# Weights split ahead in an encoder layer: stores and loads on another engine's queue

## The chip, the cores and the metric

One core of a Trainium2 chip. The metric is the device time of one run in microseconds (us). The engines are TensorE (PE in the profile, with PEld for its weight loads), VectorE (DVE), ScalarE (ACT), GpSimd (POOL) and SyncE (SP). SyncE here does nothing but issue transfers; each engine works through its own instructions in order and waits on semaphores for the others.

## What is computed

One layer of an encoder in float32, from the reference:

```python
u      = x @ W_in                        # rq, rk, rv, rg (4 x 512), aq (512), ak, av (2 x 128)
# group R: two-directional retention, 8 heads of 64, chunks of 64 here: scores * decay^|i-j|,
#          chunk states carried forward and backward, group norm per head, swish gate
# group A: windowed attention, 8 query heads on 2 key heads, +-128 tokens, sink logit, ALiBi
mix    = concat(R, A) @ W_out
h      = LN1(alpha * x + mix)
f      = SwiGLU(h) + sigmoid(h @ W_pg) * (p @ W_pe)     # FFN width 2816, p is 256 wide
out    = LN2(alpha * h + f)                             # x: (1, 1024, 1024) float32
```

## The kernel before

All large products run on TensorE as three products of operands that were split in two: `hi` is the value rounded to TensorE's reduced float32 format, `lo` is the rest, and the sum is hi·hi + hi·lo + lo·hi (`mm3`, lines L82, L83, L84). So each weight must be split before it is used: ScalarE copies `hi`, VectorE subtracts to get `lo`. For the projection weights this happens just before use (L76 and L77, with a raw tile of which there are two in flight, loaded by SyncE on L116). `w_out`, `w_pg`, `w_pe` and `p` are needed later in the kernel. They are loaded, combined, split and written back to DRAM in the shadow of the mixers: that is `presplit_out`, `presplit_gate` and `presplit_small`. Each of their steps is a `put`: ScalarE copies (L653), VectorE subtracts (L654), and a transfer of 512 KB stores both parts (L655). There are 28 puts for `w_out` (to `wod`), 28 for `w_pg` (to `pgd`), 4 for `p` (`ptd`) and 4 for `w_pe` (`ped`). A put writes into one of two operand tiles (`pro`, or `aq` and `y` tiles that are free at the time), which must be stored before a later put may reuse it.

The mixers take four head pairs in turn. First the attention of pair 0, then the retention of pair 0, then for pairs 1, 2 and 3 retention and attention together. The order of TensorE's instructions is written out by hand: `run` walks a list of steps, and each `F` in it takes its share of a queue of projection steps (one step, or tick, is three matmuls of 512 columns) that belong to the next pair. The order on ScalarE, VectorE, GpSimd and SyncE comes from a scheduler that places instructions by its own estimate; `behind` ties an instruction behind the latest projection step. Work with a due time stands in the lists `later` and `side` and is issued when the count of ticks reaches it. For pair 1 to 3 a phase has 48 ticks.

The steps that the prediction speaks of:

- `keys` (K(0), K(1)): TensorE transposes, then four ScalarE copies scaled by the decay per half (L424), into the tiles `qq` and `pt`.
- `kv` (C(0), C(1)): TensorE forms 64x64 products of decayed keys and values (L439); ScalarE (L448) and VectorE (L446) copy them out of PSUM.
- `decay_k`: for one head ScalarE makes two exponentials in a tile `sq` (L388), of which there is one; GpSimd multiplies by masks (L390) and adds (L391) into `dt`.
- `norm` (M(0), M(1)): TensorE sums squares (L528), VectorE scales the row (L530), and then, 3, 6, 9, 12 and 15 ticks later, the chain: SyncE spreads the row over partitions (L535), GpSimd raises to the power -1/2 (L538), SyncE stores to DRAM (L541), SyncE fetches it back spread (L545), VectorE scales the output with it (L549). The small tile `sn` exists once, so the second half waits for the first.
- attention: scores (L577, L578 on TensorE, L579 on VectorE, L582 on ScalarE), transposes (L617) and their copies (L622), a small copy of the denominators (L599).

In a phase every load and every store goes through SyncE's one queue, those of the norm chain and those of the puts alike; GpSimd has the masks and the powers.

Of the kernel before, what the change touches and what calls it, by code (L numbers as in the profile page):

```python
# [47 lines left out]
def layer(tc, xT, xn, w_first, w_mt, w_rv, w_out, w_pg, w_pe, pT, w_gu, w_dn,  # L48
# [89 lines left out]
    def bt(shape, tag, bufs=None, dt=F32):  # L138
        return bpool.tile(list(shape), dt, tag=tag, bufs=bufs, name=nm(tag))
# [243 lines left out]
            behind(act.activation(qd[:, h, :], cst[:, C_QD:C_QD + CH], AF.Exp, scale=lq[:, 2 * i + h:2 * i + h + 1]))  # L383

    def decay_k(i, h):
        e = bt([P, 2, CH], "sq", 1)
        for d in range(2):
            behind(act.activation(e[:, d, :], cst[:, C_B64:C_B64 + CH], AF.Exp,  # L388
                                  scale=lg[:, 8 * d + 2 * i + h:8 * d + 2 * i + h + 1]))
        pool.tensor_tensor(e, e, masks, ALU.mult)  # L390
        pool.tensor_tensor(decays[i][1][:, h, :], e[:, 0, :], e[:, 1, :], ALU.add)  # L391
# [260 lines left out]
    def put(x, o, dst):  # L652
        behind(act.activation(o[:, 0, :], x, AF.Copy))  # L653
        behind(dve.tensor_tensor(o[:, 1, :], x, o[:, 0, :].bitcast(F32), ALU.subtract))  # L654
        sp.dma_start(dst, o.bitcast(F32))  # L655

    def presplit_small(n, ops, start, at0, at1, raw=None):

        hold = []

        def load():
            r = rawt(2 * HF) if raw is None else raw
            hold.append(r)
            if n < 2:
                for j in range(4):
                    sp.dma_start(r[:, j * 2 * P:(j + 1) * 2 * P], pT[4 * n + j])
            else:
                sp.dma_start(r, w_pe[n - 2])

        def step(j):  # L670
            o = ops[j]() if callable(ops[j]) else ops[j]
            put(hold[0][:, j * HF:(j + 1) * HF], o, ptd[2 * n + j] if n < 2 else ped[n - 2, j])

        return [(ticks[0] + at, f) for at, f in ((start, load), (at0, lambda: step(0)), (at1, lambda: step(1)))]

    def presplit_out(kt, ops, start, gap, raws=()):


        hold = []

        def load():
            for j in range(2):
                r = raws[j] if j < len(raws) else rawt(2 * HF)
                sp.dma_start(r, w_out[kt + 4 * j])
                hold.extend([r[:, :HF], r[:, HF:]])

        def step(p, k, k2, i):
            x, o = hold[k], ops[i % len(ops)]
            if k2 is not None:
                behind(dve.tensor_tensor(x, x, hold[k2], ALU.add))  # L690
            put(x, o() if callable(o) else o, wod[p - 1, kt])

        todo = ((1, 0, None), (2, 2, None), (3, 3, None), (5, 0, 1), (7, 1, 3), (6, 0, 3), (4, 0, 2))
        at = gap if isinstance(gap, tuple) else [start + 5 + gap * i for i in range(7)]
        return [(ticks[0] + start, load)] + [(ticks[0] + at[i], lambda i=i, a=a: step(*a, i)) for i, a in enumerate(todo)]

    def presplit_gate():

        first, other = ([a_tile([P, 2, HF], "pre", t) for _ in range(2)] for t in ("A1", "A0"))
        ops = [a_tile([P, 2, HF], "pro", "A1", F32R) for _ in range(2)]  # L700
        n = [0]

        def load(k):
            for j in range(2):
                sp.dma_start((other if k == 1 else first)[j], w_pg[j, k])

        def steps(k):
            raw = other if k == 1 else first

            (a11, a21), (a12, a22) = ([raw[j][:, i, :] for i in range(2)] for j in range(2))  # L710

            def s(p, x, *sums):
                def f():
                    for a in sums:
                        behind(dve.tensor_tensor(*a))
                    put(x, ops[n[0] % 2], pgd[p - 1, k])
                    n[0] += 1
                return f

            return [s(1, a11), s(4, a22), s(2, a12), s(5, a22, (a22, a21, a22, ALU.add)),  # L720
                    s(7, a21, (a21, a11, a21, ALU.subtract)), s(6, a11, (a11, a22, a11, ALU.subtract)),
                    s(3, a12, (a12, a12, a11, ALU.subtract))]

        load(0)
        load(1)
        k0, k1, k2, k3 = map(steps, range(4))
        k1[0] = pair_of(k1[0], lambda: load(2))
        k3[0:0] = [lambda: load(3), lambda: None]
        at = [2 + 2.8 * k for k in range(14)] + [60 + 1.9 * k for k in range(7)] + [73 + 1.9 * k for k in range(9)]
        return [(ticks[0] + t, f) for t, f in zip(at, k0 + k1 + k2 + k3, strict=True)]  # L730
# [60 lines left out]
    with tc.manual_schedule(engines={mybir.EngineType.PE}):  # L791
# [25 lines left out]
        for i in range(1, NPAIR):  # L817
            assert i == 1 or not side, len(side)
            r = Retention(i, ytile(2 * i), states)
            a = Attention(i, ytile(2 * i + 1))  # L820
            if i == 2:
                late = [ytile(6), ytile(7)]
                ops = [twin(late[1].bitcast(F32R)), twin(bt([P, S], "aq", 3, F32R))]
                side.extend(presplit_out(2, ops, 2, 3.4, late[:1]))
                side.extend(presplit_small(0, ops[::-1], 24, 31, 34.4) + presplit_small(1, ops[::-1], 31, 37.8, 41.2))
            elif i == 3:
                op = twin(bt([P, S], "aq", 3, F32R))
                rkx = bt([P, S], "rk", 2)
                more = []

                def spare_op(k):
                    if not more:
                        more.append(twin(bt([P, S], "rk", 2, F32R)))
                    return more[0] if k % 2 else op

                side.extend(presplit_out(3, [op, op, op, op, lambda: spare_op(1), op, lambda: spare_op(1)], 3,
                                         (8, 13.5, 19, 24.5, 30, 33.5, 37), [rkx]))
                side.extend(presplit_small(2, [op, lambda: spare_op(1)], 40, 43.5, 46.5, rkx))
                side.extend(presplit_small(3, [op, lambda: spare_op(1)], 46, 50, 53))
            G = [(f, i + 1, *x) for f, x in ((decay_q, ()), (decay_k, (0,)), (decay_k, (1,)))] if i + 1 < NPAIR else \  # L840
                [(lambda: None,)] * 3
            run([K(0), F, K(1), sco(0), F, *V, C(0), C(1), F, sco(1), S_(0, 0), F, trn(0), sco(2), S_(0, 1), F, trn(1),
                 sco(3), S_(1, 0), F, val(0), val(1), S_(1, 1), F, trn(2), sco(4), F, trn(3), sco(5), Q(0), F, val(2), val(3),
                 (r.scores,), F, trn(4), sco(6), Q(1), F, trn(5), sco(7), F, (r.out,), E(0), E(1), F, G[0], F, M(0), G[1], F,
                 val(4), val(5), G[2], F, trn(6), M(1), F, trn(7), F], 48)
            V = [val(6), val(7)]
# [1223 lines left out]
```

## Time and profile before

| | |
|---|---|
| time, median of 3 runs | 1168.02 us (1165.01 to 1168.27) |
| the profiled execution | 1168.96 us, span 1167.2 us |
| granted clock of TensorE | 0.998 |
| hardware queue (SyncE, ScalarE) | 200.11 MB, 49.6% of 16 engines |
| software queue (GpSimd) | 17.31 MB, 8.4% |

The span is the time from the first to the last instruction; 1.76 us lie around it. A row of a timeline gives start, duration, engine, line, operation, output and inputs by the program's names, a count, and in brackets the idle time of that engine before it with what released it. Names in the profile have no buffer numbers. SPq and POOLq are the two engines' issuing of transfers; "to landing" is the time from the issue to the arrival of the last byte.

The attention of pair 0 runs from about 33 to 118 us, the retention of pair 0 to about 160 us, pairs 1, 2 and 3 to about 345 us, and everything after the mixers from 360 us on.

### The profile page before, as it was taken

The page shows a single profiled execution, that of the slowest core. Times are in us where ns is not written, and L with a number is a line of the kernel's source. Part 1 is how long each engine was busy: PE and PEld are TensorE (multiplying, and loading weights), DVE is VectorE, ACT ScalarE, POOL GpSimd, SP SyncE. Part 2 cuts the span into 40 slices and gives each one's busy share as a digit, 9 for nine tenths or more (in the row PEclk, how much of TensorE's full clock was granted, in tenths as well). Part 3 has the DMA queues.
Part 4 walks back from the last instruction along what each step waited for, and adds up shares of the span by engine and source line. Part 5 has one row for each costly group of instructions (what it writes and reads, how often), then busy time and mean ns, then how long its engine had stood idle before and what let it go on. Part 6 is the DMA issues. An engine that isn't in the chain of part 4 may idle for free.

```text
span 1167.2 us, 19086 instructions
## 1 busy us (share of the span) xinstructions
PE 1151.9 (99%) x6978; PEld 965.8 (83%) x6978; DVE 895.7 (77%) x1687; ACT 564.4 (48%) x1162; POOL 105.1 (9%) x118
## 2 busy tenths in 40 slices
PE   9999999999999999999999999999999999999997
PEld 7888878777888888888888888888888888888886
DVE  5556678594858898948999988888888876774778
ACT  5645367666546366214444433443344445552462
POOL 2000010102010021000000000000000011124242
PEclk9999999999999999999999999999999999999999
DMA  6346777666567955756322332332223289999978
GB/s 251 103 159 214 258 241 232 211 210 194 154 216 241 365 178 185 269 193 210 112 96 98 115 107 98 103 134 101 100 73 136 83 249 344 348 236 217 256 172 233
DMA packets 88863, 218.64 MB, mean 187 GB/s; under 512 B 12544, under 2 KB 20928, under 8 KB 88768
## 3 DMA queue, kind: packets, MB, share of 16 engines
q1 hardware_dynamic: 79984, 200.11, 49.6%
q0 software_dynamic: 8784, 17.31, 8.4%
q8 instruction: 55, 0.90, 0.3%
q14 instruction: 40, 0.33, 0.1%
HBM read 143.35 MB, written 62.19 MB: 176 GB/s over the span
## 4 chain that ended last, share of the span: by engine, by line
PE 89%; issue 4%; DMA 3%; DVE 2%; ACT 1%; SPq 1%; POOL 0%; DVEq 0%; POOLq 0%; ACTq 0%
PE bmm L875 8%; PE bmm L874 8%; PE bmm L876 8%; PE bt L874 6%; PE bt L875 6%; PE bt L876 6%; PE bmm L82 4%; PE bmm L84 4%; PE bmm L83 4%; PE bs L876 4%; PE bs L875 4%; PE bs L874 4%; PE bo L876 4%; PE bo L875 4%; PE bo L874 4%
## 5 line engine op out<-in xcount | busy, mean ns | idle before, releaser
L82 PE MATMUL bmm<-H,w 128*128 128x512 f32 x240 | 97.2, 405 | 0.1
L84 PE MATMUL bmm<-H,w 128*128 128x512 f32 x240 | 94.0, 392 | 0.5 <-issue 0.5
L83 PE MATMUL bmm<-H,w 128*128 128x512 f32 x240 | 94.0, 392 | 0.0
L1474 ACT ACTIVATE ev<-ev 128x512 f32<-128x512 f32 x42 | 26.5, 630 | 105.0 <-DVE ev L1503 91.8
L1648 POOL DMA_DIRECT2D h0b<-in_w_dn x24 | 21.6, 900 | 537.7 <-DVE ev L1454 503.6
L82 PEld LDWEIGHTS bmm<-H,w 128*128 128x128 f32 x240 | 45.2, 188 | 12.2 <-issue 1.9
L84 PEld LDWEIGHTS bmm<-H,w 128*128 128x128 f32 x240 | 45.0, 188 | 10.2
L83 PEld LDWEIGHTS bmm<-H,w 128*128 128x128 f32 x240 | 45.1, 188 | 7.8
L582 ACT ACTIVATE sc<-sc,st 128x384 f32<-128x384 f32 (+1 forms) x64 | 37.3, 586 | 17.1 <-DVE st L579 17.0
L579 DVE CUSTOM_DVE_ANT_0 sc<-cst,bs,nskb 128x384 f32<-128x384 f32 (+1 forms) x64 | 35.2, 575 | 7.0 <-PE bs L578 6.9
L1503 DVE TENSOR_TENSOR ev<-ev,bt 128x512 f32<-128x512 f32 x44 | 30.0, 682 | 12.5 <-PE bt L876 12.5
L622 ACT ACTIVATE ptr<-bt 128x384 f32<-128x384 f32 (+1 forms) x64 | 26.5, 456 | 25.5 <-PE bt L617 25.4
L1454 DVE TENSOR_TENSOR ev<-ev,bs 128x256 f32<-128x256 f32 x63 | 25.5, 416 | 15.6 <-PE bs L876 14.7
L1476 DVE TENSOR_TENSOR ev<-ev 128x512 f32<-128x512 f32 x42 | 29.0, 691 | 10.5 <-ACT ev L1474 9.0
L77 DVE TENSOR_TENSOR w<-raw,w 128x512 fp32r<-128x512 f32 x34 | 23.0, 687 | 17.3 <-ACT w L76 16.7
L874 PE MATMUL bmm<-H,u 128*128 128x512 f32 x92 | 36.1, 392 | 0.0
L875 PE MATMUL bmm<-H,u 128*128 128x512 f32 x92 | 36.0, 392 | 0.0
L876 PE MATMUL bmm<-H,u 128*128 128x512 f32 x92 | 35.8, 389 | 0.0
L874 PE MATMUL bmm<-H,w 128*128 128x512 f32 x84 | 32.9, 392 | 0.0
L875 PE MATMUL bmm<-H,w 128*128 128x512 f32 x84 | 32.9, 392 | 0.0
L876 PE MATMUL bmm<-H,w 128*128 128x512 f32 x84 | 32.7, 389 | 0.0
L1454 DVE TENSOR_TENSOR ev<-ev,bo 128x256 f32<-128x256 f32 x70 | 28.3, 416 | 5.2 <-PE bo L876 4.5
(832 smaller groups left out, 3836.8 us busy)
## 6 DMA issues: line engine op xcount, KB each, us to landing
ad<-ev SPq DMA_DIRECT2D x33, 512.0 KB, 2.6
pgd<-pro SPq DMA_DIRECT2D x28, 512.0 KB, 3.3
raw<-in_w_gu SPq DMA_DIRECT2D x22, 512.0 KB, 4.0
ln<-in_w_gu SPq DMA_DIRECT2D x22, 512.0 KB, 4.6
raw<-ad SPq DMA_DIRECT2D x40, 256.0 KB, 6.2
ln<-ad SPq DMA_DIRECT2D x37, 256.0 KB, 6.3
H<-in_w_dn SPq DMA_DIRECT2D x33, 256.0 KB, 9.2
wod<-aq SPq DMA_DIRECT2D x16, 512.0 KB, 2.7
```

The costliest lines, as they stand in the source:

```text
L82: pe.matmul(o, lh, rh, start=start, stop=False)
L83: pe.matmul(o, lh, rl, start=False, stop=False)
L84: recent[0] = pe.matmul(o, ll, rh, start=False, stop=stop).ins.name
L579: dve.tensor_tensor_reduce(sc[g][:, :nk], cst[:, tc0:tc0 + nk], b[:, :nk], slope(i, g), nskb[:, 2 * i + g:2 * i + g + 1], ALU.add, ALU.min ...
L582: act.activation(sc[g][:, :nk], sc[g][:, :nk], AF.Exp, bias=st_[:, 0, j, g:g + 1], scale=-1.0, accum_out=st_[:, 2, j, g:g + 1])
L622: act.activation(p_[:, :hi - lo, :], tb[:, :hi - lo, :], AF.Copy)
L874: pe.matmul(o, lh, rh, start=start, stop=False, skip_group_check=True)
L875: pe.matmul(o, lh, rl, start=False, stop=False, skip_group_check=True)
L876: pe.matmul(o, ll, rh, start=False, stop=stop, skip_group_check=True)
L1454: dve.tensor_tensor(out_, x, b, ALU.add)
L1476: dve.tensor_tensor(c[:, 1, :], c[:, 0, :], c[:, 1, :], ALU.mult)
L1503: dve.tensor_tensor(get(name), ev[left][:, m, :], right, ALU.add)
```

## The change

The change has four parts. The stores of all puts and the loads of `w_out`, `w_pg`, `p` and `w_pe` are issued by GpSimd instead of SyncE. The two heads' exponentials of a pair go into halves of one `sq` tile. The loads of `p` and their puts come later in pair 2's phase. In pair 1's phase, where no steps of an earlier pair are left over (`V` is empty), one more `F` stands behind K(1), so the 48 ticks are shared by 21 of them instead of 20.

```diff
     def decay_k(i, h):
-        e = bt([P, 2, CH], "sq", 1)
+        if h == 0:
+            decays["e"] = bt([P, 2, 2, CH], "sq", 1)
+        e = decays["e"][:, h]
         for d in range(2):
             behind(act.activation(e[:, d, :], cst[:, C_B64:C_B64 + CH], AF.Exp, ...
...
     def put(x, o, dst):
         behind(act.activation(o[:, 0, :], x, AF.Copy))
         behind(dve.tensor_tensor(o[:, 1, :], x, o[:, 0, :].bitcast(F32), ALU.subtract))
-        sp.dma_start(dst, o.bitcast(F32))
+        pool.dma_start(dst, o.bitcast(F32))
...
             if n < 2:                                   # presplit_small: load
                 for j in range(4):
-                    sp.dma_start(r[:, j * 2 * P:(j + 1) * 2 * P], pT[4 * n + j])
+                    pool.dma_start(r[:, j * 2 * P:(j + 1) * 2 * P], pT[4 * n + j])
             else:
-                sp.dma_start(r, w_pe[n - 2])
+                pool.dma_start(r, w_pe[n - 2])
...
-                sp.dma_start(r, w_out[kt + 4 * j])      # presplit_out: load
+                pool.dma_start(r, w_out[kt + 4 * j])
...
-                sp.dma_start((other if k == 1 else first)[j], w_pg[j, k])      # presplit_gate: load
+                pool.dma_start((other if k == 1 else first)[j], w_pg[j, k])
...
-                side.extend(presplit_small(0, ops[::-1], 24, 31, 34.4) + presplit_small(1, ops[::-1], 31, 37.8, 41.2))
+                side.extend(presplit_small(0, ops[::-1], 28.5, 34, 37.4) + presplit_small(1, ops[::-1], 39.5, 44.5, 47.9))
...
-            run([K(0), F, K(1), sco(0), F, *V, C(0), C(1), F, ...
+            run([K(0), F, K(1), *([] if V else [F]), sco(0), F, *V, C(0), C(1), F, ...
```

All lines behind `decay_k` have a number higher by 2 in the changed kernel.

In ScalarE's queue, at the passage from the retention of pair 0 to pair 1, stand the exponentials of pair 1's second head (`sq`), copies of pair 1's attention queries (`aq`), splits of projection weights (`w`), the decayed key copies (`qq`, `pt`) and puts (`pro`). Before:

```order
L388 ACTIVATE sq_1645<-cst,lg 128x64 x2
L256 ACTIVATE aq_468<-bmm_1599 64x512
L76 ACTIVATE w_1674<-raw_1669 128x512
L424 ACTIVATE qq_1663<-bt_1658,kd 128x4x64
L653 ACTIVATE pro_1139<-pre_1137 128x512
L256 ACTIVATE aq_1594<-bmm_1599 64x512
L424 ACTIVATE qq_1663<-bt_1658,kd 128x4x64
L424 ACTIVATE pt_1666<-bt_1658,kd 128x4x64
L653 ACTIVATE pro_1140<-pre_1138 128x512
L424 ACTIVATE pt_1666<-bt_1658,kd 128x4x64
L424 ACTIVATE qq_1663<-bt_1685,kd 128x4x64 x2
L424 ACTIVATE pt_1666<-bt_1685,kd 128x4x64 x2
```

And in the changed kernel, from the exponentials of the first head on:

```order
L390 ACTIVATE sq_1621<-cst,lg 128x64 x2
L76 ACTIVATE w_1669<-raw_1667 128x512
L390 ACTIVATE sq_1621<-cst,lg 128x64 x2
L256 ACTIVATE aq_468<-bmm_1598 64x512
L76 ACTIVATE w_1672<-raw_1667 128x512
L426 ACTIVATE qq_1661<-bt_1656,kd 128x4x64 x2
L256 ACTIVATE aq_1593<-bmm_1598 64x512
L426 ACTIVATE pt_1664<-bt_1656,kd 128x4x64 x2
L426 ACTIVATE qq_1661<-bt_1683,kd 128x4x64 x2
L426 ACTIVATE pt_1664<-bt_1683,kd 128x4x64 x2
```

The two puts have left this stretch, and the second head's exponentials follow the first head's with one weight split between them. On TensorE nine projection matmuls stand between K(1) and kv(0) before, behind the first attention scores, and fifteen in the changed kernel, nine of them ahead of those scores.

In GpSimd's queue, at the passage from pair 1 to pair 2, stand masks and sums of the decays of pair 2 (`sq`, `dt`) and the two powers of pair 1's norm chain (`sn`). Before:

```order
L390 TENSOR_TENSOR sq_2314<-sq_2314,masks 128x128
L391 TENSOR_TENSOR dt_2288<-sq_2314 128x64
L390 TENSOR_TENSOR sq_2353<-sq_2353,masks 128x128
L391 TENSOR_TENSOR dt_2288<-sq_2353 128x64
L538 TENSOR_TENSOR sn_2312<-sn_2312,cst 128x8
L538 TENSOR_TENSOR sn_2387<-sn_2387,cst 128x8
```

In the changed kernel, with a load of `w_out` ahead and one in the middle:

```order
L686 DMA raw_2460<-in_w_out 128x1024
L657 DMA pgd<-pro_1139 128x1024
L657 DMA pgd<-pro_1138 128x1024
L392 TENSOR_TENSOR sq_2312<-sq_2312,masks 128x128 x2
L393 TENSOR_TENSOR dt_2293<-sq_2312 128x64 x2
L657 DMA pgd<-pro_1139 128x1024
L540 TENSOR_TENSOR sn_2310<-sn_2310,cst 128x8
L657 DMA pgd<-pro_1138 128x1024
L686 DMA y_2428<-in_w_out 128x1024
L657 DMA pgd<-pro_1139 128x1024
L540 TENSOR_TENSOR sn_2384<-sn_2384,cst 128x8
```

Three puts' stores stand ahead of the first power, and two stores and a load between it and the second.

In SyncE's queue at the same place, from the first spread to the first fetch, before:

```order
L535 DMA sn_2312<-rb_2310 64x1x8 x2
L655 DMA pgd<-pro_1140 128x1024
L655 DMA pgd<-pro_1139 128x1024
L655 DMA pgd<-pro_1140 128x1024
L602 DMA adn<-y_1657 8x128
L655 DMA pgd<-pro_1139 128x1024
L541 DMA rnd<-sn_2312 128x8
L606 DMA y_1657<-adn 64x4x128
L655 DMA pgd<-pro_1140 128x1024
L535 DMA sn_2387<-kv_2385 64x1x8 x2
L606 DMA y_1657<-adn 64x4x128
L545 DMA rb_2313<-rnd 64x512 x2
```

And in the changed kernel:

```order
L537 DMA sn_2310<-rb_2308 64x1x8 x2
L604 DMA adn<-y_1655 8x128
L543 DMA rnd<-sn_2310 128x8
L608 DMA y_1655<-adn 64x4x128
L537 DMA sn_2384<-kv_2382 64x1x8 x2
L608 DMA y_1655<-adn 64x4x128
L547 DMA rb_2311<-rnd 64x512 x2
```

The five stores of puts between the spread and the fetch are gone; the order of the rest is the same.

More of the change, by code (lines that the diff above doesn't have):

```diff
@@ L841, in layer @@
                 [(lambda: None,)] * 3
-            run([K(0), F, K(1), sco(0), F, *V, C(0), C(1), F, sco(1), S_(0, 0), F, trn(0), sco(2), S_(0, 1), F, trn(1),
+            run([K(0), F, K(1), *([] if V else [F]), sco(0), F, *V, C(0), C(1), F, sco(1), S_(0, 0), F, trn(0), sco(2), S_(0, 1), F, trn(1),
                  sco(3), S_(1, 0), F, val(0), val(1), S_(1, 1), F, trn(2), sco(4), F, trn(3), sco(5), Q(0), F, val(2), val(3),
```

## Prediction

> **What bounds the kernel now.** I read the page's first part, then the windows by stage, then TensorE's waits in the mixers, then the timelines around each wait. Page, busy time of TensorE:
>
> ```profile
> span 1167.2 us, 19086 instructions
> PE   1151.9 (99%) x6978; PEld 965.8 (83%) x6978; DVE 895.7 (77%) x1687; ACT 564.4 (48%) x1162; POOL 105.1 (9%) x118
> ```
>
> TensorE is idle for 1167.2 − 1151.9 = 15.3 us. The change adds and removes no matmul, so it can only move those 15.3 us. The stages (start:end, length, then PE, PEld, DVE, ACT, POOL, clock, DMA share, GB/s):
>
> ```profile
> 164.00:225.00 61.00, 57.51 (x613) 46.81 (x612) 46.43 (x103) 42.98 (x107) 7.37 (x9) 1.00 0.64 212
> 225.00:285.00 60.00, 57.73 (x634) 47.69 (x632) 40.68 (x95) 38.74 (x100) 6.01 (x6) 1.00 0.64 206
> 360.00:1150.00 790.00, 789.97 (x3887) 669.46 (x3886) 638.90 (x1154) 352.57 (x670) 70.27 (x76) 1.00 0.56 178
> ```
>
> From 360 us to 1150 us nothing is idle (0.03 us). The two stages in which pairs 1 and 2 are mixed lose 3.49 and 2.27 us. TensorE's waits from 118 to 360 us (line waited, releaser: us, times, longest):
>
> ```profile
> PE bt L439 <- ACT pt L424: 1.9, 2, 1.1
> PE bs L577 <- DVE pt L446: 1.7, 1, 1.7
> PE bt L617 <- ACT ptr L622: 0.8, 1, 0.8
> PE bt L617 <- ACT y L599: 0.6, 1, 0.6
> PE bs L577 <- DVE st L579: 0.5, 1, 0.5
> PE bmm L84 <- issue: 0.5, 1, 0.5
> PE bs L577 <- DVE pt L481: 0.2, 1, 0.2
> ```
>
> They add up to 6.2 us: all that the change can win. The rest of the 15.3 lies in the start and the tail, which it does not touch.
>
> **The change, part by part.**
>
> *Wait 1, 1.9 us: keys of pair 1.* ScalarE is late with the four decayed key copies (L424). ScalarE, GpSimd and TensorE rows just before:
>
> ```profile
> 163.13 0.59 ACT L388 ACTIVATE sq<-cst,lg 128x64 f32<-128x64 f32 x2 [1.31 <-POOL dt L391]
> 165.12 0.62 ACT L653 ACTIVATE pro<-pre 128x512 fp32r<-128x512 f32 x1
> 167.11 0.63 ACT L653 ACTIVATE pro<-pre 128x512 fp32r<-128x512 f32 x1
> 161.98 1.12 POOL L391 TENSOR_TENSOR dt<-sq 128x64 f32<-128x64 f32 x1
> 166.56 0.39 PE L82 MATMUL bmm<-H,w 128*128 128x512 f32 x1
> 166.79 0.40 PE L83 MATMUL bmm<-H,w 128*128 128x512 f32 x1
> ```
>
> The second head's exponentials stand 1.31 us until GpSimd has read the first head's; two puts (0.62 and 0.63) sit between the key copies. With halves of one buffer the 1.31 goes, and in the new order no put stands there: ScalarE is up to 2.56 us earlier. TensorE also gets six more matmuls ahead of kv(0), 15 for 9; one starts 0.23 us after the other, so it arrives 1.4 us later. Together 3.9 us against a wait of 1.9. The matmuls alone would leave 0.5, so the gain lies between 1.4 and 1.9; I take 1.75.
>
> *Wait 2, 0.8 us: pair 1, after the evictions.* ScalarE before its L622:
>
> ```profile
> 215.09 0.63 ACT L653 ACTIVATE pro<-pre 128x512 fp32r<-128x512 f32 x1 [3.75 <-DMA pgd<-pro]
> 217.50 0.59 ACT L388 ACTIVATE sq<-cst,lg 128x64 f32<-128x64 f32 x2 [0.49 <-POOL dt L391]
> ```
>
> ScalarE stands 3.75 us in a put whose operand buffer is still being stored, then 0.49 us on the decay buffer. The new queue has the stores ahead of the w_out load, and the decay buffer holds both heads. But a put still stands just ahead of the first L622, and a second one between the two L622 rows, which costs another 0.63 there. Gain 0 to 0.8; I take 0.6, since 4.2 us of stall go against 0.63.
>
> *Wait 3, 1.7 us: the norm chain of pair 1.* It runs spread (SyncE L535), pow (GpSimd L538), store (L541), fetch (L545), scaling (VectorE L549); behind the last stand the kv copies L446 that TensorE awaits.
>
> ```profile
> 219.01 1.65 POOL L538 TENSOR_TENSOR sn<-sn,cst 128x8 f32<-128x8 f32 x1
> 216.47 5.33 SPq L655 DMA_DIRECT2D pgd<-pro  x3
> 223.29 0.40 SPq L541 DMA_DIRECT2D rnd<-sn  x1
> 228.01 1.25 SPq L545 DMA_DIRECT2D rb<-rnd  x2
> 220.76 0.69 DVE L654 TENSOR_TENSOR pro<-pre,pro 128x512 fp32r<-128x512 f32 x1
> 233.79 0.75 DVE L549 SCALAR_TENSOR_TENSOR y<-y,gn,rb 128x512 f32<-128x512 f32 x1 [2.69 <-DMA rb<-rnd]
> rb<-rnd SPq DMA_DIRECT2D x8, 128.0 KB, 3.6
> DMA to landing us min/median/max: 1.8/2.4/3.4
> ```
>
> The pow ends at 220.66, but SyncE, held by stores that wait for VectorE, sends the result only at 223.29, and the fetch at 228.01. VectorE then idles 2.69 us, of which TensorE feels 1.7. In the new order GpSimd holds one more put's store ahead of the pow: that put's subtraction ended at 220.76 + 0.69 = 221.45, its store's issue takes 0.9 (below), so the pow ends near 224.0, 3.3 us later than now. SyncE has no stores left and sends at once, at 224.0 instead of 223.29. From there 0.3 of issue and 2.4 of landing (the last row, DMAs of the sn tile) give 226.8; with the second spread's issues in between I put the fetch at 227.3 and its second half at 227.9. It lands 3.6 us later (median) at 231.5, or, if as slowly as now (5.8 after the first issue), at 233.1. VectorE's L549 thus comes 0.7 to 2.3 us earlier and the wait falls to between 0 and 1.0; I take 0.5, a gain of 1.2. What is late next is still this chain, now by GpSimd's order instead of SyncE's.
>
> *Wait 4, 0.6 us: first gate.* ScalarE stands for a projection weight that SyncE asked for late:
>
> ```profile
> 279.51 1.16 ACT L76 ACTIVATE w<-raw 128x512 fp32r<-128x512 f32 x2 [1.51 <-DMA raw<-in_w_mt]
> 274.93 0.54 SPq L116 DMA_DIRECT2D raw<-in_w_mt  x1
> ```
>
> The second load of p now starts at tick 39.5 instead of 31 and leaves the raw slot to this weight, which SyncE, without stores, asks for as soon as the slot is free. Gain 0 to 0.6; I take 0.5, since 1.51 us of lateness is little against the several us by which the slot comes free earlier.
>
> The remaining 0.5, 0.5 and 0.2 (VectorE's own backlog, and an issue) stay.
>
> *What GpSimd's queue costs.* 64 stores and 26 further DMA calls move, loads of p counted as calls of four. Nearest rows (a group, a tile's row, landing times, a tile's row):
>
> ```profile
> L1648 POOL DMA_DIRECT2D h0b<-in_w_dn x24 | 21.6, 900 | 537.7 <-DVE ev L1454 503.6
> L655 SPq DMA_DIRECT2D pgd<-pro x28: 319/326/872, 124.1 to 225.6; - x28
> pgd<-pro SPq DMA_DIRECT2D x28, 512.0 KB, 3.3
> acc<-u POOLq DMA_DIRECT2D x5, 512.0 KB, 4.6
> L1808 POOL DMA_DIRECT2D acc<-R x12: 874/880/1456, 1033.6 to 1079.3; - x12
> ```
>
> An issue costs 0.90 us on GpSimd for 0.33 on SyncE: about 90 × 0.9 = 80 us on an engine busy for 105.1 us of 1167.2, so it is hidden as a total. What isn't hidden is order. A put's buffer returns after 0.9 + 4.6 instead of 0.33 + 3.3, up to 1.9 us later. ScalarE's wait for it is now
>
> ```profile
> ACT pro L653 <- DMA pgd<-pro: 13.5, 10, 3.8
> 199.87 1.92 SPq L705 DMA_DIRECT2D pre<-in_w_pg  x2
> 206.07 1.23 ACT L653 ACTIVATE pro<-pre 128x512 fp32r<-128x512 f32 x2
> ```
>
> and 13.5 us of it cost TensorE only wait 2. One more place: the last w_pg block, loaded at 199.87 and first put at 206.07. The new order has that put about ten ScalarE rows earlier, ahead of attention work, and its load behind a store in GpSimd's queue, so ScalarE may stand there 0 to 2 us; TensorE would feel 0 to 1, I take 0.4, nearer to the lower end because 13.5 us of such waits now reach it so seldom. For the pows of pairs 2 and 3, which show no wait now, 0 to 1 in all; I take 0.3, as at most two puts are queued ahead of them. The second half of pair 1's chain is inside wait 3.
>
> **Sum.** 1.75 + 0.6 + 1.2 + 0.5 = 4.05 won, 0.7 lost. The modelled matmul ends hide a bit more in each closed wait (0.39 shown for a step of 0.23, so 0.16 each, 0.4 for the two or three that close fully). Net −3.7 us. The profiled execution took 1168.96 (span 1167.2 and 1.76 around it), which gives 1165.2; it lies 0.94 above the median of the runs, 1168.02, from which 1164.3 follows.
>
> **A page against the trace.** VectorE's split beside GpSimd's issue, late in the kernel:
>
> ```profile
> 1037.66 0.69 DVE L77 TENSOR_TENSOR h<-raw,h 128x512 fp32r<-128x512 f32 x1
> 1037.30 0.88 POOL L1648 DMA_DIRECT2D h0b<-in_w_dn  x1 [0.99 <-issue]
> ```
>
> The issue took its usual 0.88 us beside a two-input VectorE operation, and that its usual 0.69. The Trainium skill (SBUF — State Buffer, "SBUF: two separate sides") says that GpSimd cannot write a DMA's descriptors while VectorE holds the port pair that the two share, in a two-port mode, and gives about 620 ns grown to 3100. By that figure the store ahead of each pow would come some 2.5 us later, in three pairs 7.5, less a slack of 1 us in each 4.5, and the sum of −3.7 would become +0.8, 1168.8. The two rows don't show it.
>
> **Rivals.**
>
> *B, all waits go and no new ones come:* 6.2 − 1.2 (what stays) + 0.5 hidden = 5.5, so 1162.5, or 1161 if the remaining backlog closes too. For it: SyncE no longer stands behind puts anywhere. Against it: the pow is queued later than now.
>
> *C, the pow keeps wait 3 alive and the last w_pg block costs 1:* waits 1 and 4 alone, 2.25 less 1.0: 1166.8. For it: the 3.3 us by which the pow ends later, against 2.6 us that SyncE wasted.
>
> *D, the stores are not earlier at all:* DMA share was 0.64 in both stages, and what held buffers was the transfer, not the issue. Then only the decay halves and the six matmuls count, 1.4, less the 0.9 us issues: about 1167.5. The Trainium skill (DMA: Bandwidth & Descriptors, "Issuing engines are not separate DMA queues") says just that: another issuing engine saves only its sequencer's time. By it wait 2 stays; wait 3, which was SyncE's time, would go in any case.
>
> *E, slower:* GpSimd's queue is in order. If issues stretch (the L1808 row has 1.46 for 0.88, and L391 above took 1.12) or two puts stall ahead of each pow, every pair's L549 is late, and VectorE stops the kv copies or the scores. The 2.69 us of VectorE's idling cost 1.7, so 1 us is slack. It decides from a pow some 3.6 us later than its fetch can bear in three pairs: 3 × 2.6 = 7.8 lost against 4.4 won, +3.4, 1171.5 and above; I put it at 1172.
>
> **How the numbers follow.** A measurement of this kernel tells 0.3%, 3.5 us, from no change: faster is below 1164.5, slower above 1171.5. The forecast (1163 to 1166.5) has 0.44, of it 0.32 below 1164.5; B 0.14; C 0.18; D 0.10; E 0.14, of it 0.12 above 1171.5 (stretched issues are 0.04 of it). Faster 0.32 + 0.14 = 0.46, slower 0.12, same 0.42. The range 1161 to 1169.5 leaves out E and the best of B.
>
> **What would show it.** Right: between 164 and 225 us TensorE idle for 1.2 or less instead of 3.5; no wait of kv(0) on the key copies; L390 without a wait on GpSimd; SyncE's result store right behind the pow; kv copies without a wait of TensorE over 0.6. Wrong: a wait of TensorE around the last w_pg block, GpSimd's issues over 1.2 us on average, the scaling still over 2 us late, or any loss beyond 360 us, where I expect none.

## The result: 1.4% slower, and where the time went

| | before | after |
|---|---|---|
| median of 6 runs | 1168.17 us (1165.01 to 1169.34) | 1185.68 us (1180.48 to 1186.57) |
| ratio | | 1.0141, 95% interval [1.0117, 1.0165] |
| profiled execution, its span | 1168.96, 1167.2 | 1181.72, 1179.9 |

The profiled execution of after lies 4 us below its median, so the profiles show 12.7 of the 17.5 us. Page of after, busy times and the two queues that carry data:

```profile
PE 1155.7 (98%) x6978; PEld 968.4 (82%) x6978; DVE 894.7 (76%) x1687; ACT 563.8 (48%) x1162; POOL 152.4 (13%) x208
q1 hardware_dynamic: 67024, 156.06, 38.7%
q0 software_dynamic: 20976, 61.35, 18.7%
```

44 MB moved from the hardware queue to GpSimd's. The packets' time on both together is 57.4% of the longer span for 58.0% of the shorter one, 677 us both times: the bytes did not become dearer. TensorE's idle time rose from 15.3 to 24.2 us, and its busy time by 3.8 us with the same 6978 matmuls. The windows of after (columns as in the prediction) and the first one of before:

```profile
118.00:164.00 46.00, 40.49 (x457) 33.01 (x457) 26.11 (x50) 16.93 (x32) 9.77 (x20) 0.93 0.79 268
164.00:225.00 61.00, 56.64 (x581) 45.91 (x579) 45.98 (x103) 42.63 (x109) 14.32 (x23) 0.97 0.57 190
360.00:1150.00 790.00, 788.36 (x3879) 667.79 (x3878) 637.29 (x1151) 351.68 (x668) 65.78 (x71) 1.00 0.56 179
```

```profile
118.00:164.00 46.00, 45.92 (x490) 37.42 (x489) 31.76 (x57) 22.51 (x46) 1.72 (x3) 1.00 0.76 271
```

The first stage, the retention of pair 0, lost nothing before (0.08 us) and loses 5.5 now. TensorE's waits of after from 118 to 385 us:

```profile
PE bmm L82 <- ACT rq L246: 5.5, 1, 5.5
PE bs L579 <- DVE pt L483: 3.4, 3, 2.2
PE bt L622 <- DVE st L593: 3.1, 1, 3.1
PE bt L878 <- DVE H L77: 1.6, 1, 1.6
```

Two of 0.4 follow. The waits 1 to 4 of the prediction are not in it. Others stand there, and the longest is for an eviction (a copy out of PSUM) at the end of pair 0, where ScalarE copies half of the next pair's retention queries (L246). ScalarE there, before and then after:

```profile
145.64 0.63 ACT L653 ACTIVATE pro<-pre 128x512 fp32r<-128x512 f32 x1 [2.01 <-DMA pgd<-pro]
146.43 0.59 ACT L246 ACTIVATE rq<-bmm 64x512 f32<-64x512 f32 x1 [0.16 <-DVE rq L245]
147.76 0.59 ACT L246 ACTIVATE rq<-bmm 64x512 f32<-64x512 f32 x1
150.24 0.63 ACT L653 ACTIVATE pro<-pre 128x512 fp32r<-128x512 f32 x1 [1.89 <-DMA pgd<-pro]
```

```profile
146.63 0.63 ACT L655 ACTIVATE pro<-pre 128x512 fp32r<-128x512 f32 x1 [2.20 <-DMA pgd<-pro]
152.02 0.63 ACT L655 ACTIVATE pro<-pre 128x512 fp32r<-128x512 f32 x1 [4.75 <-DMA pgd<-pro]
152.67 0.59 ACT L246 ACTIVATE rq<-bmm 64x512 f32<-64x512 f32 x1
156.79 0.59 ACT L246 ACTIVATE rq<-bmm 64x512 f32<-64x512 f32 x1 [0.55 <-DVE rq L245]
```

Before, the two evictions follow one another and the puts that must wait for their buffer stand behind them. After, one more put has moved ahead of the first eviction, and another (at 155.60) between the two. The one ahead stands 4.75 us for a store, and the eviction behind it, and TensorE behind that, stand with it. The granted clock (PEclk, third figure from the end) there, and after the wait of 3.1 us:

```profile
150.50:156.50 6.00, 3.18 (x8) 2.51 (x9) 2.92 (x5) 2.48 (x4) 0.53 (x1) 0.50 0.91 302
197.50:201.00 3.50, 3.50 (x11) 3.01 (x11) 2.85 (x7) 1.57 (x4) 0.73 (x2) 0.52 0.69 247
```

Both times the clock is at half. One projection matmul follows the other after 0.43 us there (at 199) and after 0.23 where the clock is back at 1.00 (at 203). TensorE works for 3.2 and 3.5 us at that clock; about half of it, 3.3 us, would be saved at full clock, by this estimate most of the extra 3.8 us of busy time. The waits of 2.2 (at 270) and 1.6 us (at 369) cost no clock in this profile.

### The profile page after: what moved, and what is told of

Same layout as the page of the kernel before. It is cut to its first block, busy times and chain, and to the rows that moved or that the text cites. A ratio compares the mean times of both kernels' runs of the same rounds, so it can differ in the third digit from the quotient of the medians.

```text
span 1179.9 us, 19117 instructions
## 1 busy us (share of the span) xinstructions
PE 1155.7 (98%) x6978; PEld 968.4 (82%) x6978; DVE 894.7 (76%) x1687; ACT 563.8 (48%) x1162; POOL 152.4 (13%) x208
## 4 chain that ended last, share of the span: by engine, by line
PE 67%; DVE 1%; DMA 1%; issue 1%; POOL 0%; SPq 0%; DVEq 0%; POOLq 0%
PE bmm L877 8%; PE bmm L876 8%; PE bmm L878 8%; PE bt L878 6%; PE bt L877 6%; PE bt L876 6%; PE bs L878 4%; PE bs L877 4%; PE bs L876 4%; PE bo L878 4%; PE bo L877 4%; PE bo L876 4%; DMA kv<-rnd 0%; DMA rnd<-sn 0%; POOL sn L540 0%
## 5 line engine op out<-in xcount | busy, mean ns | idle before, releaser
L656 DVE TENSOR_TENSOR pro<-pre,pro 128x512 fp32r<-128x512 f32 x28 | 19.2, 689 | 20.9 <-ACT pro L655 18.5
L77 DVE TENSOR_TENSOR w<-raw,w 128x512 fp32r<-128x512 f32 x34 | 23.1, 688 | 15.4 <-ACT w L76 15.0
```

## Which part of the change costs

All runs below are compared with the kernel before on the same chip. First one part at a time.

**The queues put back** (halves of `sq`, the additional F and the later p stay), timed, and once more for a profile:

```diff
-        pool.dma_start(dst, o.bitcast(F32))          # put; the loads of w_pg, w_out, p, w_pe alike
+        sp.dma_start(dst, o.bitcast(F32))
```

> The changed kernel with stores and loads back on SyncE's queue (decay halves, extra share behind K(1) and later p stay). Theory 1 (order: with the stores on GpSimd the scheduler sets a put ahead of the eviction L246, ScalarE stands in it, TensorE waits 5.5 us and its clock falls): no such wait, TensorE's wait on the key copies gone, 1163 to 1167 us. Theory 2 (the transfers themselves land later when issued by GpSimd): the same, 1163 to 1167. Theory 3 (the loss comes from the shifted due times and the extra share, which delay the norm chain and the scores): 1175 us or more, with the waits at the norm chain.

> The same kernel as in the run with the queues back on SyncE (time like before), for a profile. If the decay halves and the extra share do what the prediction said, TensorE's wait on the key copies (1.9 us near 168 us) is at most 0.3 us, L390 stands behind no wait on GpSimd; and the wait behind the w_mt load (0.6 us near 282 us) is gone. Since the time did not change, 2 us or more of other waits must have come in their place, or the kv copies' wait (1.7 us) grown.

Measured: 1167.18 us, ratio 0.9994 [0.9984, 1.0004], and 1169.34 in the profiled execution. The whole loss hangs on the queues. The other three parts are worth nothing together that these runs could tell, though waits 1 to 4 are not in its trace. TensorE still waits 5.5 us in all from 118 to 385 us, for 6.2 before. TensorE's longest waits there:

```profile
PE bs L579 <- DVE st L581: 1.9, 2, 1.2
PE bt L622 <- DVE st L593: 1.5, 1, 1.5
```

The waits near 180 and 189 us are at the scores of pair 1: TensorE comes to them earlier and finds VectorE behind with them. That it waits there because it comes earlier is a reading of the two traces, not a test of its own.

**Only the stores; only the loads; only the loads of w_pg and w_out; both, with nothing else of the change**, each on the kernel before:

```diff
     def put(x, o, dst):
...
-        sp.dma_start(dst, o.bitcast(F32))
+        pool.dma_start(dst, o.bitcast(F32))          # stores, queue
...
-                    sp.dma_start(r[:, j * 2 * P:(j + 1) * 2 * P], pT[4 * n + j])
+                    pool.dma_start(r[:, j * 2 * P:(j + 1) * 2 * P], pT[4 * n + j])      # loads, queue; w_pe alike
...
-                sp.dma_start(r, w_out[kt + 4 * j])
+                pool.dma_start(r, w_out[kt + 4 * j])          # loads, loads_w, queue; w_pg alike
```

> The kernel before with only the puts' stores on GpSimd. Theory 1: the put stands ahead of L246 here too, TensorE waits 3 to 6 us near 150 us, 1175 to 1185 us. Theory 2 (loads and stores of 512 KB behind one another in GpSimd's queue): loads stay on SyncE, so the stores land in some 3.3 us as before and the time is 1168 to 1171. Theory 3: 1166 to 1170.

> The kernel before with only the loads on GpSimd, stores on SyncE. Theory 1: L246 stands ahead of the put as before, no new wait of TensorE over 1 us, 1165 to 1170 us. Theory 2: 1166 to 1172, the loads landing up to 2 us later. Theory 3: 1166 to 1170.

> The kernel before with the loads of w_pg and w_out on GpSimd, those of p and w_pe on SyncE as before, all stores on SyncE. With all loads on GpSimd TensorE waited 3.9 us near 268 us for a fetch of the attention's denominators that landed 4.4 us after its issue, beside p's loads that GpSimd had sent at once. Theory 2: that wait falls to 1.5 us or less; 1169 to 1174 us. Theory 4: it stays, 1176 to 1179 us.

> The kernel before with stores and loads on GpSimd and nothing else (no decay halves, no extra share, p as before). Theories 1 and 2: the queue is the whole of the loss, 1180 to 1188 us. Theory 3 (due times and the extra share): 1170 to 1176 us.

| | median us | ratio |
|---|---|---|
| stores | 1185.12 | 1.0154 [1.0117, 1.0192] |
| loads | 1177.89 | 1.0101 [1.0084, 1.0118] |
| loads of w_pg and w_out | 1172.86 | 1.0044 [1.0027, 1.0060] |
| stores and loads | 1188.47 | 1.0180 [1.0137, 1.0223] |

Both parts cost, and they do not add up. With the stores alone the wait for L246 is 5.24 us, at 152. With the loads alone the order at that place is as before, and TensorE waits later, for the denominators on their way through DRAM (`adn`; the loads alone; VectorE, then TensorE):

```profile
266.98 0.69 DVE L637 TENSOR_TENSOR y<-bo,y 128x512 f32<-128x512 f32 x1 [3.21 <-DMA y<-adn]
268.32 0.69 PE L577 MATMUL bs<-k,aq 128*128 128x384 f32 x1 [3.89 <-DVE pt L481]
```

GpSimd sends four loads of p at 253.81; SyncE stores the denominators at 256.68 and fetches them at 262.54, just behind a load of `w_out` that GpSimd sent at 261.73. Without the loads of p on that queue this wait is gone; no run tells whether by their transfers or by the order that changed with them.

## Three repairs of the largest place

My first theory was local: the put ahead of L246 (six puts moved later), or the w_pg load that GpSimd now sends at 141.86 us instead of SyncE at 147.40, beside the stores (the load tied to a later tick), or both.

```diff
-        at = [2 + 2.8 * k for k in range(14)] + ...
+        at = [2 + 2.8 * k for k in range(8)] + [32 + 2.8 * k for k in range(6)] + ...      # late_puts, late_both
...
-                pool.dma_start((other if k == 1 else first)[j], w_pg[j, k])
+                d = pool.dma_start((other if k == 1 else first)[j], w_pg[j, k])          # late_load, late_both
+                if k == 2:
+                    behind(d)
...
-        k1[0] = pair_of(k1[0], lambda: load(2))
+        k1[5] = pair_of(k1[5], lambda: load(2))
```

> The changed kernel with six puts of w_pg's second block due later (ticks 32 to 46 instead of 24.4 to 38.4), so that the first eviction L246 stands ahead of the put that it waited behind. Theory 1: the wait of 5.5 us goes with its loss of clock, 1170 to 1177 us; what is left are the waits at the norm chain of pairs 0 and 3 and at the scores of pair 2 (3.1, 1.6, 2.2 us in the changed kernel). Theory 2: ScalarE stands in another put at another eviction, 1181 us or more. Theory 3: 1181 us or more.

> The changed kernel with the load of w_pg's third block (1 MB) tied to tick 35.6 of pair 0's retention instead of 21.6; ScalarE's order is unchanged, a put still stands ahead of the eviction L246. Theory 1 (order of ScalarE): TensorE still waits 4 us or more on L246, 1180 us or more. Theory 2 (crowding: SyncE, standing in stores, used to hold this load back to 147 us; freed, it starts near 142 us beside three stores, which then land in 5.5 to 8.1 us instead of 3.3 to 4.6, and ScalarE stands in its puts): stores near 141 to 148 us land in under 5 us, the wait on L246 is at most 1.5 us, the state of pair 0 comes out 5 us earlier, 1171 to 1177 us.

> The changed kernel with both: w_pg's third block loaded at tick 35.6, and six puts of its second block due at ticks 32 to 46, so that no put stands ahead of the first eviction L246. Alone, the late load left 3.5 us of the 5.5 us wait on L246 and the late puts left 2.9. Combined theory (order and crowding each make a part): the wait is at most 1 us, pair 0's state is read (first L506) by 153 us, 1171 to 1178 us, the waits at the norm chains of pairs 0 and 1 left. If ScalarE's put cycle on GpSimd's queue is slow whatever the order: a wait of 2.5 us or more stays, 1180 us or more.

Measured: 1182.82, 1184.92 and 1185.06 us (ratios 1.0133, 1.0146, 1.0133), and the wait for L246 2.88, 3.46 and 2.90 us instead of 5.5. Each half of the theory had hold of something, and neither mends the time: other waits grow (L593's to 3.87 and 4.30 us in the first two, L483's from 3.4 to 5.9 us in all in the third). Then all of w_pg went back to SyncE, with the rest left on GpSimd:

```diff
-                    put(x, ops[n[0] % 2], pgd[p - 1, k])
+                    put(x, ops[n[0] % 2], pgd[p - 1, k], sp)          # and its loads on sp
```

> The changed kernel with w_pg's loads and stores back on SyncE; those of w_out, p and w_pe stay on GpSimd. Theory 1 and theory 2: pair 0's retention and pair 1 run as in the kernel before (L246 ahead of the put, w_pg's load held back by stores), no wait over 1.5 us before 215 us; what is left of the loss lies in pairs 2 and 3, 1168 to 1176 us. If moving any bulk transfer to GpSimd costs by itself (theory 4): 1177 us or more.

Measured: 1176.78 us, 1.0074 [1.0045, 1.0103]. The first stage loses nothing again (0.11 us), and between 164 and 205 us TensorE idles 3.43 us (2.61 before); but 3.75 us are at 219 (for VectorE's L532) and 2.37 at 266 (L483). The loss is not of one place.

## Is it the queue itself? The norm chain's small transfers

The opposite test: stores and loads stay on SyncE, and only the short transfers of the norm chain (4 KB, and fetches of 128 KB) go to GpSimd; the second run has the halves, the additional F and the later p besides.

```diff
-                sp.dma_start(home, sm[:, 1])
+                pool.dma_start(home, sm[:, 1])          # spread and fetch alike
```

> The reverse of the change: the kernel before, with bulk stores and loads on SyncE, and the six small transfers of each norm chain (spread, store, fetch) on GpSimd's queue. If the crowding theory is right (SyncE's standing in stores spaces the bulk transfers, and only the chain suffers from it), the wait of 1.7 us on the kv copies falls to 0.5 or less, nothing new over 1 us, 1163 to 1167 us. If any use of GpSimd's queue costs (theory 4): 1170 us or more.

> The same with the changed kernel's decay halves, extra share and later loads of p, queues of bulk on SyncE. If the gains add: 1161 to 1166 us, faster than before by 0.2% or more. Theory 4: 1170 us or more.

Measured: 1187.5 us, 1.0162 [1.0140, 1.0184], and 1186.96, 1.0156 [1.0142, 1.0170]. The dearest place is the last chain, just behind the mixers (first run; GpSimd, VectorE, TensorE):

```profile
369.72 1.04 POOL L545 DMA_DIRECT2D kv<-rnd  x2 [4.09 <-DMA rnd<-sn]
376.92 0.75 DVE L549 SCALAR_TENSOR_TENSOR y<-y,gn,kv 128x512 f32<-128x512 f32 x1 [10.11 <-DMA kv<-rnd]
378.32 0.80 PE L876 MATMUL bt<-raw,H 128*128 128x512 f32 x1 [10.20 <-DVE H L77]
```

GpSimd stands 4.09 us until 4 KB have landed, and the fetch takes 7. Every use of GpSimd's queue had cost by then, so I took the queue itself for the cause. Six more runs tested that against what had changed with it each time: the order that the scheduler writes for the other engines.

## Order or queue

**pinned** issues the stores from GpSimd and holds ScalarE, VectorE, GpSimd's arithmetic and SyncE to the order of the kernel before, instruction by instruction (TensorE's was the same anyway). SyncE issues a store of 1 KB where it issued the put's store, so that it waits in the same places. **order_only** leaves every transfer on SyncE and takes from the stores kernel the order on ScalarE and VectorE; the order of SyncE's transfers was left to the scheduler, and is not quite that of before. **tokens** has the 1 KB stores and the order free.

```diff
     def put(x, o, dst):
...
-        sp.dma_start(dst, o.bitcast(F32))
+        nc.gpsimd.dma_start(dst, o.bitcast(F32))                                  # pinned, tokens
+        sp.dma_start(tok[tokens[0]], o[0:2, 1, 0:P].bitcast(F32))                 # pinned, tokens
...
+    for e in ORDER:                                               # pinned: of before; order_only: of stores
+        order = [k for k in ORDER[e] if start[e] <= k < len(notes[e])]
+        for a, b in zip(order, order[1:]):
+            tc.add_manual_dep(notes[e][b], notes[e][a].name, mybir.DependencyInfo(
...
```

> The kernel before with the puts' stores issued by GpSimd, and the order of instructions on TensorE, ScalarE, VectorE and SyncE held to that of the kernel before, instruction by instruction; where SyncE issued a put's store it now issues a 1 KB store of the same operand, so that it waits at the same places. With the order free this cost 17 us (1185.1). If GpSimd's queue itself is what costs (its transfers take longer than SyncE's among the same neighbours): most of it stays, 1180 to 1187, and ScalarE waits longer for the put buffers than the 13.5 us of before. If the cost is the order that the scheduler writes for the other queue: within 0.3% of before, 1165 to 1172. About half of each, 1174 to 1179, if both count.

> The other half: every transfer stays on SyncE's queue, and only the order on ScalarE and VectorE is that of the kernel whose stores are on GpSimd's queue (1185.1). If the order is the cause: 1178 to 1187, with TensorE waiting some 4 to 5 us for the last evictions of pair 0's queries near 150 us, as there. If the queue is the cause: 1165 to 1171, since SyncE's stores land in time for that order.

> The stores on GpSimd's queue, the order on ScalarE and VectorE free again, but SyncE keeps a 1 KB store in the place of each put's store, so it still stands until the operand is ready and can't run ahead to its next loads. If SyncE's running ahead (its bulk loads beside the stores) makes the cost: 1168 to 1173. If ScalarE's order, or the queue, makes it: 1180 to 1187.

| stores from | order on ScalarE, VectorE | median us | ratio |
|---|---|---|---|
| GpSimd | free (the stores kernel) | 1185.12 | 1.0154 [1.0117, 1.0192] |
| GpSimd | free, SyncE held (tokens) | 1183.49 | 1.0133 [1.0116, 1.0149] |
| SyncE | as in the stores kernel (order_only) | 1183.28 | 1.0131 [1.0113, 1.0149] |
| GpSimd | as before (pinned) | 1172.56 | 1.0047 [1.0031, 1.0064] |

The cleanest pair is tokens and pinned: the same transfers from the same queues, and only the order differs, 1183.49 against 1172.56 us. With the order of before, 0.5% is left (just above what pinned's expectation gave for order alone); it belongs to the queue, or to the 64 stores of 1 KB that pinned adds on SyncE, which no run separates there. SyncE's running ahead is not shown to cost anything in sum (1.0133 against 1.0154).

order_only shows that an order costs as much, 1.3%, with no transfer moved at all. But it is not the same loss throughout. At the end of pair 0 order_only waits as the stores kernel does; from 285 to 360 us it loses more, where TensorE idled 0.57 us before (stores, then order_only):

```profile
285.00:360.00 75.00, 72.89 (x731) 59.51 (x731) 48.65 (x108) 41.77 (x105) 14.97 (x20) 1.00 0.54 172
285.00:360.00 75.00, 68.45 (x689) 56.16 (x688) 48.02 (x106) 40.89 (x102) 4.26 (x3) 0.98 0.53 165
```

2.11 us idle in stores, 6.55 in order_only. Ahead of the first of its waits after 290 us, ScalarE stands 5.78 us for a weight that SyncE asked for at 291.82. So the 1.3% and the 0.5% may not be added up to the whole as if they were its two parts.

In the pinned and order_only runs the instructions of ScalarE, VectorE and SyncE carry one line, that of the helper which notes them, so they are told apart by names. ScalarE of order_only, then of pinned, around the evictions at the end of pair 0:

```profile
150.06 0.63 ACT L58 ACTIVATE pro<-pre 128x512 fp32r<-128x512 f32 x1 [3.85 <-DMA pgd<-pro]
150.71 0.59 ACT L58 ACTIVATE rq<-bmm 64x512 f32<-64x512 f32 x1
```

```profile
147.72 0.59 ACT L58 ACTIVATE rq<-bmm 64x512 f32<-64x512 f32 x1 [3.58 <-DVE rq L58]
148.99 0.59 ACT L58 ACTIVATE rq<-bmm 64x512 f32<-64x512 f32 x1
154.85 0.63 ACT L58 ACTIVATE pro<-pre 128x512 fp32r<-128x512 f32 x1 [4.61 <-DMA pgd<-pro]
```

In order_only the put at 150.06 stands 3.85 us ahead of the evictions, and TensorE waits 4.4 us, though SyncE sent the stores ahead of it when it did before (144.19 against 144.36). In pinned a put stands even longer, 4.61 us, but behind both evictions; TensorE waits 1.4. What a stall costs is set by what is queued behind it. How long it is still depends on the landing: in tokens a put stands ahead of the first eviction too, but SyncE, held, sends the next w_pg load at 148.07 instead of 140.69 us (stores), and TensorE waits 2.68 us there instead of 5.24. Why the scheduler wrote the puts earlier is not in a trace; that it places instructions by its own estimate, and that only the stores' queue differed, is all that is known.

**The queues by themselves**: a kernel that leaves out the layer, and times one store from each of three queues, alone and with four loads of 512 KB sent by SyncE.

> No layer: it computes nothing of the reference, and its own time means nothing beside the others. It times transfers one by one, six times each, from three queues (SyncE, ScalarE, GpSimd): a store of 512 KB (a put's), a store of 128 rows of 32 B (the chain's), a fetch of 2 x 128 KB spread over partitions (the chain's), each alone, then with four loads of 512 KB from SyncE: ahead of them or behind them on SyncE, or beside them on another queue. If GpSimd's queue is slow by itself: alone, it lands the row store at least 1 us later than SyncE. If it is only a matter of who is ahead: alone within 0.5 us of each other; ahead of the loads on SyncE close to alone, about 2.5 us for the put and 2 us for the row; beside them on GpSimd's queue 4 us or more for the put and 3 us or more for the row; and ScalarE's queue beside them like GpSimd's. Behind them on SyncE the longest, 7 us or more.

Issues (name, issuing queue, count, size, median us from issue to landing):

```profile
put_alone_sp<-big SPq DMA_DIRECT2D x6, 512.0 KB, 2.6
put_alone_pool<-big POOLq DMA_DIRECT2D x6, 512.0 KB, 2.9
put_ahead_sp<-big SPq DMA_DIRECT2D x6, 512.0 KB, 2.9
put_behind_sp<-big SPq DMA_DIRECT2D x6, 512.0 KB, 8.4
put_beside_pool<-big POOLq DMA_DIRECT2D x6, 512.0 KB, 7.5
put_beside_act<-big ACTq DMA_DIRECT2D x6, 512.0 KB, 4.8
row_alone_sp<-big SPq DMA_DIRECT2D x6, 4.0 KB, 1.4
row_alone_pool<-big POOLq DMA_DIRECT2D x6, 4.0 KB, 1.7
row_ahead_sp<-big SPq DMA_DIRECT2D x6, 4.0 KB, 1.4
row_behind_sp<-big SPq DMA_DIRECT2D x6, 4.0 KB, 6.2
row_beside_pool<-big POOLq DMA_DIRECT2D x6, 4.0 KB, 4.4
row_beside_act<-big ACTq DMA_DIRECT2D x6, 4.0 KB, 3.4
```

Alone, GpSimd's queue lands 0.3 us later, within the 0.5 us that the expectation gave for queues that are alike. Beside bulk loads it makes a large difference who is ahead: in one queue a store ahead of the loads is all but undisturbed (2.9 us) and one behind them lands late (8.4), and a store on GpSimd's queue lands nearer to the one behind than to the one ahead (7.5). ScalarE's queue did better than expected, 4.8 for 7.5: the two are not alike. The Trainium skill (DMA: Bandwidth & Descriptors, "Issuing engines are not separate DMA queues") says that transfers from any engine end up interleaved on the same 16 DMA engines and that another issuing engine saves only the time of issuing. The rows agree with the first half (7.5 against 2.9 alone) and not with the second: 4 KB behind the loads take 6.2 us, and from another engine 3.4 or 4.4.

**The whole change and the chain, with the order held.** after_pinned is the changed kernel, with all its transfers on GpSimd, in the order of the same kernel with its queues put back; chain_pinned is the chain kernel in the order of before.

```diff
-        pool.dma_start(dst, o.bitcast(F32))          # after_pinned, in the order of q_back
+        moved.dma_start(dst, o.bitcast(F32))         # moved issues on GpSimd
...
-                sp.dma_start(home, sm[:, 1])
+                moved.dma_start(home, sm[:, 1])          # chain_pinned, in the order of before; spread and fetch alike
```

> The changed kernel, all its transfers on GpSimd's queue as in it, but the order on ScalarE and VectorE, and of what is left on SyncE, held to that of the same kernel with its queues put back (which measured 1167.2). Order, for the puts' stores, was worth some 12 of 17 us; if that holds for the whole change: 1169 to 1175 instead of 1185.7, and TensorE's wait of 5.5 us for the last evictions of pair 0 falls below 2. If in the whole change the loads on the second queue or SyncE's running ahead weigh more than the order: 1177 to 1186.

> The kernel before with only the norm chain's small transfers on GpSimd's queue (with its order free: 1187.5), and the order on ScalarE, VectorE and of the rest of SyncE held to that of the kernel before. These transfers are short and waited for, not long and reused: if the order is the cause here too: 1166 to 1173. If it is their longer way (waits of 4.3 to 6.8 us for 4 KB to land, beside bulk loads that SyncE has sent ahead): most stays, 1179 to 1188, and the wait of some 10 us near 378 us for the last chain is still there.

Measured: after_pinned 1175.62 us, 1.0074 [1.0056, 1.0092]; chain_pinned 1172.67, 1.0050 [1.0031, 1.0069]. For the whole change the order is about half: 1.41% becomes 0.74%, which lies between the two expectations. For the chain it is two thirds: 1.62% becomes 0.50%. The wait for L246 is down to 1.7 in after_pinned; what is left there (TensorE's longest waits):

```profile
PE bo L706 <- DVE y L58: 2.4, 1, 2.4
...
PE bmm L281 <- ACT rq L58: 1.7, 1, 1.7
```

The last chain in chain_pinned (GpSimd, VectorE):

```profile
354.68 1.04 POOL L58 DMA_DIRECT2D kv<-rnd  x2 [4.09 <-DMA rnd<-sn]
362.83 0.75 DVE L58 SCALAR_TENSOR_TENSOR y<-y,gn,kv 128x512 f32<-128x512 f32 x1 [5.04 <-DMA kv<-rnd]
```

The 4 KB land as slowly as with the order free (GpSimd stands the same 4.09 us), and the fetch takes 8 us instead of 7. But the fetch goes out 15 us earlier, and the 10.20 us are gone. About half of the 15 us would be the waits of 3.6 and 3.5 us that TensorE has in the pairs before in the chain kernel and not in chain_pinned. So the theory of the slow queue fell as the main cause of the loss of the stores and of the chain; in the whole change about half is left. The rest of 0.5 to 0.7% with the order held is put down to that queue's later landings beside bulk loads by the difference between the kernels and the rows above; no run shortens them, so this is argued, not shown. No version beat the kernel before.

## Why the prediction was wrong, point by point

*Waits 1 to 4* did go from TensorE, as forecast. (Behind wait 3, VectorE's scaling still stands 2.81 us for its fetch, 2.69 before, which the prediction had named as a sign of being wrong; TensorE no longer feels it.) But their 4.05 us are not won even with the queues put back (0.9994: between −1.9 and +0.5 us of 1167). The sum took each closed wait as time won; TensorE, earlier by it, met VectorE's backlog in the next scores (1.9 and 1.5 us), a cover the prediction did not price. It had counted VectorE's own backlog among what "stays".

*What GpSimd's queue costs.* The issue was mis-sized, to no effect: a put's store takes GpSimd

```profile
L657 POOL DMA_DIRECT2D pgd<-pro x28: 533/533/638, 125.3 to 234.1; - x28
```

0.53 us, not 0.90. The step that failed is the next one: "What isn't hidden is order" was priced at 0.4 us for one put and 0.3 for the pows. It looked at the last w_pg block; the largest loss, 5.5 us, is in the second block, at the end of pair 0, where the order on ScalarE had not been compared. With the order held the whole change costs 0.74% instead of 1.41%: order was worth about 8 us, not 0.7. And it took "13.5 us of it cost TensorE only wait 2" as a property of such waits. They are now

```profile
ACT pro L655 <- DMA pgd<-pro: 19.3, 8, 4.8
```

5.8 us longer in all for these tiles, but one of them has an eviction behind it, and that alone is TensorE's 5.5 us. By order_only (4.4 us with SyncE's stores) and pinned (1.4 with GpSimd's) the order decides there, and the landing sets the length.

*"It can only move those 15.3 us"* left out the clock. TensorE's busy time rose by 3.8 us with the same matmuls, most of it at half clock behind the new waits.

*Rival E* had the sign and a chance of 0.14, and another mechanism: neither stretched issues nor puts ahead of the pows. The pow of pair 0's second half chain, which runs in pair 1's phase, waited for the spread's data, not for its turn in GpSimd's queue, and VectorE waited for the fetch (GpSimd, VectorE, TensorE):

```profile
183.17 1.64 POOL L540 TENSOR_TENSOR sn<-sn,cst 128x8 f32<-128x8 f32 x1 [5.92 <-DMA sn<-kv]
190.92 0.75 DVE L551 SCALAR_TENSOR_TENSOR y<-y,gn,kv 128x512 f32<-128x512 f32 x1 [2.84 <-DMA kv<-rnd]
197.37 0.27 PE L622 MATMUL bt<-cst,st 128*8 128x128 f32 x1 [3.12 <-DVE st L593]
```

Its 1172 was 13.7 us short: there was no term for the retention of pair 0.

*The port pair.* By the rule of the Trainium skill that the prediction priced (SBUF — State Buffer, "SBUF: two separate sides") the issues would have become longer; they were 0.53 to 0.64 us, so nothing of it shows here. The rule is for VectorE in a two-port mode, and the same section says that a TENSOR_TENSOR has none; the split that the prediction looked at, L77, is one, so its row could not have told.

*Beyond 360 us* no loss was forecast; 1.6 us are there (788.36 busy of 790), the last chain's.

## What to carry to other kernels

Where a scheduler writes the order by its estimates, moving a transfer to another queue is a change of order on every engine: compare the order of all engines over the whole stage, and price each wait by what is queued behind it, not by its length. To tell the two apart, hold the order and change the queue, and then the other way round; that told in five runs what twelve others had not. A single queue also protects: a store issued ahead of four loads landed after 2.9 us, and after 7.5 us beside the same loads from GpSimd's queue.

## What the runs showed of the hardware

Behind some idle times of TensorE the granted clock is at half for some 3 us of work; in the changed kernel this followed the ones of 5.5 and 3.1 us and not those up to 2.2. The length does not decide alone, as two other runs show, one of loads_w with a wait of 1.98 us, one of chain_halves with 2.95 (the matmul behind the wait, then the window of 3 us):

```profile
172.37 1.78 PE L439 MATMUL bt<-rv,qq 64*64 64x64 f32 x56 [1.98 <-ACT pt L424]
172.00:175.00 3.00, 2.63 (x98) 2.63 (x102) 0.67 (x3) 1.89 (x6) 0.00 (x0) 0.56 0.63 176
241.28 0.45 PE L579 MATMUL bs<-k,aq 128*128 128x384 f32 x1 [2.95 <-DVE pt L448]
241.00:244.00 3.00, 2.72 (x15) 2.43 (x16) 3.00 (x9) 1.01 (x3) 0.00 (x0) 1.00 0.47 190
```

After 1.98 us the clock was at 0.56, after 2.95 us at 1.00. The Trainium skill (TensorE: Matmul & The Clock Gate, "HAM oscillation — how this bites in real kernels") gives about 3.4 us as the idle time that must not be passed; here 1.98 us cost once and 2.95 us once did not.

A store of 512 KB beside four loads landed after 4.8 us from ScalarE's queue but 7.5 from GpSimd's, where both took 2.6 to 2.9 alone.
